# Where an attention kernel's filler matmuls stand, and when transposed activations leave PSUM

## The chip, the cores and the metric

The kernel runs on one core of a Trainium2 chip. The metric is the device time of one execution in microseconds (us). The same execution leaves a trace of every instruction on each engine: TensorE (PE, with its weight loads shown apart as PEld), VectorE (DVE), ScalarE (ACT), GpSimd (POOL) and SyncE (SP), whose queue issues the DMAs.

## The reference

One layer of an encoder over 1024 tokens of width 1024, all in float32:

```
h = x @ w_in                                # qa ka va qb kb vb ga gb
y_a = banded softmax attention(qa, ka, va, rel_bias) @ w_proj_a    # 8 heads of 64, branch A
y_b = stick-breaking attention(qb, kb, vb) @ w_proj_b              # 8 heads of 64, branch B
mix = (sigmoid(ga + b_a) * y_a + sigmoid(gb + b_b) * y_b) @ w_out
x   = LN(alpha * x + mix)
g, u = split(x @ w_ffn_in)
out = LN(alpha * x + (silu(g) * u) @ w_ffn_out)
```

Branch A lets a 64-token chunk attend to itself and the 8 chunks before it. Branch B computes weights beta_ts * prod(1 - beta_tj) with beta = sigmoid(q.k / 8), strictly causal. The tokens are held in reversed order, so that both masks reach forward.

## The kernel before, in words

Every product that needs float32 accuracy is made of three matmuls: an operand is split into a high part (ACT casts it) and a low part (DVE or POOL subtracts the high part from the raw value), and high*high, high*low and low*high are summed in PSUM. `split` (L110, L111) is the pair of instructions that does it. The large projections run as seven half-size products in place of eight (`pair_steps`, `product`).

The stages in order of time: the input projections (to 333 us), the 16 attention heads (333 to 643 us; 0 to 7 are branch A, 8 to 15 branch B), the gated branch projections and the output projection (to 773 us), the first layer norm with its transposes (in the same stretch), the feed-forward network (from 773 us).

A framework places the instructions. It takes the order in which the program issues them as a priority and gives each engine the first one that its own estimate of durations holds ready; only instructions tied with `keep_in_program_order` keep their order on their engine. Buffers are drawn from pools: `slot` gives one of a few 128x1024 tiles of a tag, `bank` one of the eight PSUM banks (`mm` 2, `sc` 2, `tr` 3, `pv` 1). A buffer comes free when its last reader is done, and whoever wants it waits for that.

**The heads.** A loop over `vsteps` has 12 steps (`pos`) for each head: 8 for the first half of the queries (`g` = 0), 4 for the second. A step emits, in this order: the score units that `LEAD` calls for (`wunits`; a score unit is one 128-query block; in branch A, step 2 emits the first block of the *next* head, in two cuts of 320 columns), postponed work (`later`), the step's transposes of weights (`turn`, L807, evacuated by `split` into `pt`), half of its filler matmuls, the product with V of the step two or three back (`mult`, L820 and L821, into the one `pv` bank), and the rest of its fillers. At the end of each half head ACT copies the `pv` bank out (L839); only then can the next half's first `mult` start.

In branch A a score block is reduced by DVE out of its `sc` bank (L738), exponentiated by ACT (L744), divided by POOL (L749) and only then transposed. In branch B, ACT takes two sigmoids out of the `sc` bank (L776, L777), DVE scans (L779, L782) and POOL multiplies (L784).

**The fillers.** 480 matmuls that do not depend on the heads' chains are dealt out among the steps: the gates 10 to 15 (48 matmuls each, `gate`, L598) and branch A's output projection (192, `yAps`, L896). `FILL` says how many each head gets (18 in heads 0 to 6, 34 in head 7, 38 to 40 in branch B), `AHEAD` is 8 at the start; `goal` is the running count and `fill_until` emits fillers up to it. While gate i runs, the weights of gate i+1 are split once, at the start of its second half (`half_way`): one ACT cast of 128x1024 (L549) and one POOL subtraction of 128x1024 (L550), both tied.

**The transposed x.** After the first layer norm (`layer_norm`, `norm_1`), `x1_operands(hf)` transposes half of the tokens: per `kt` two PSUM banks of four 128x128 transposes each (L1178). Each bank is read three times: ACT casts the high half (L110), DVE subtracts for the low half (L111), ACT copies the raw value (L1188 for hf 0, L1197 for hf 1). `x1_operands(0)` comes after token tile 4 of the second column half of the output projection (`ops`, L117, L118 and L120, 24 matmuls a tile); `x1_operands(1)` runs between the two products of the first feed-forward column block (`plainhl`, `plainhr`).

Of the kernel before, what the change touches and what calls it, by code (L numbers as in the profile page):

```python
# [11 lines left out]
F32 = mybir.dt.float32  # L12
F32R = mybir.dt.float32r
AF = mybir.ActivationFunctionType
ALU = mybir.AluOpType
# [20 lines left out]
LAG = 2  # L36
LEAD = ((6, 8, 9, 9, 10, 10, 11, 11, 12, 12, 13, 13), (7, 8, 9, 9, 10, 10, 11, 11, 12, 12, 13, 14))

FILL = (18, 18, 18, 18, 18, 18, 18, 34, 40, 40, 39, 39, 40, 38, 38, 38)
AHEAD = 8  # L40


# [6 lines left out]
def hybrid_trunk_kernel(ctx: ExitStack, tc, x, xt, w_first, w_v, w_in, b_gate, rel_bias, w_proj,  # L49
# [59 lines left out]
    def split(dst_h, dst_l, src):  # L109
        return (nc.scalar.copy(dst_h, src),  # L110
                nc.vector.tensor_tensor(dst_l, src, dst_h.bitcast(F32), ALU.subtract))  # L111
# [426 lines left out]
    def begin_w(srcs, name, raw, hl, lo_eng, in_turn=False):  # L538
        r = raw(f"wr_{name}")
        srcs = srcs if isinstance(srcs, list) else [(slice(0, 1024), srcs)]  # L540
        for cs, src in srcs:
            ins = dma(r[:, cs], src)
            if in_turn:
                tc.keep_in_program_order(ins)

        def end(tied=False):
            hi = hl(f"wh_{name}", F32R)
            lo = hl(f"wl_{name}", F32R)
            for ins in (nc.scalar.copy(hi, r),  # L549
                        lo_eng.tensor_tensor(lo, r, hi.bitcast(F32), ALU.subtract)):  # L550
                if tied:
                    tc.keep_in_program_order(ins)
            return hi, lo
        return end

# [35 lines left out]
    def gate(i, w, half_way, freed=None):  # L591
        gt = slot("gt", f"gate{i}")
        acc = [bank("mm", f"gps{i}_{hf}") for hf in range(1 if freed is None else 2)]

        def part(hf, k):
            ks = slice(k * P, (k + 1) * P)
            for j, (lw, rx) in enumerate(((w[0], xh), (w[0], xl), (w[1], xh))):
                mm(acc[hf], lw[:, ks], rx[k][:, (LO, HI)[hf]], start=(k == j == 0),  # L598
                   stop=(k == KT - 1 and j == 2))
                yield 1.0  # L600

        def take(hf):
            nc.scalar.copy(gt[:, (LO, HI)[hf]], acc[hf])

        if freed is None:
            for hf in range(2):
                if hf:
                    acc.append(bank("mm", f"gps{i}_1"))
                    half_way()
                for k in range(KT):  # L610
                    yield from part(hf, k)
                take(hf)
        else:
            half_way()
            for k in range(6):
                for hf in range(2):
                    yield from part(hf, k)
                freed(k)
            for hf in range(2):
                for k in (6, 7):  # L620
                    yield from part(hf, k)
                    if k + hf == 7:
                        freed(7)
                take(hf)
                freed(6 + 2 * hf)
        dma(g_dr[i], gt)
# [226 lines left out]
        return steps  # L853


    def fill_all():
        w = first_w
        got = []
        for i in range(first_gate, 15):
            end = begin_gate(i + 1, nc.gpsimd)  # L860
            yield from gate(i, w, lambda: got.append(end(True)))
            w = got.pop()
        end = begin_proj(0, 0)
        ends = {}

        pieces = []

        def freed(k):
            if k < 4:
                ends[k] = begin_y(k)  # L870
            if 1 < k < 6:
                ends[k - 2](LO)
                pieces.append(lambda: ends[k - 2](HI))
            elif k > 5:
                pieces.pop(0)()

        yield from gate(15, w, lambda: None, freed)
        w = end()
        gates = {0: begin_gA(0)}
        for cc in range(4):  # L880
            if cc < 3:
                end = begin_proj(0, cc + 1)
            for j in range(2):
                c = 2 * cc + j
                t = gates.pop(c)
                squash(t, c, 0)
                if c < 7:
                    gates[c + 1] = begin_gA(c + 1)
                for hf, cs in enumerate((LO, HI)):
                    acc = bank("mm", f"yAps{c}_{hf}")  # L890
                    if j == 1 and hf == 0 and cc < 3:
                        got.append(end())
                    for k in range(4):
                        ks = slice(j * HW + k * P, j * HW + (k + 1) * P)
                        for n, (lw, rx) in enumerate(((w[0], yh), (w[0], yl), (w[1], yh))):
                            mm(acc, lw[:, ks], rx[k][:, cs], start=(k == n == 0),  # L896
                               stop=(k == 3 and n == 2))
                            yield 1.0
                        if k == 1 and pieces:
                            pieces.pop(0)()  # L900
                    nc.vector.tensor_tensor(t[:, cs], acc, t[:, cs], ALU.mult)
                if c < KEEP:
                    dma(m_dr[c], t)
                else:
                    kept[c] = t
                if c == 0:
                    end_y = begin_y(4)
                elif c < 3:
                    end_y((LO, HI)[c - 1])
            if cc < 3:  # L910
                w = got.pop()
# [94 lines left out]
    for si, (hd, g, st, box) in enumerate(vsteps):  # L1006
        hidx, pos = si // nhead, si % nhead
        if hidx < 14 and pos == 8:
            load_qk(heads[hidx + 2])
            if hidx < 6:  # L1010
                later.append([3, heads[hidx + 2]["end_bias"]])
        if pos == 4:
            if hidx < 15:
                load_v(heads[hidx + 1])
            else:
                next_w = begin_proj(1, 3)()
                end_11, end_21 = (begin_wo(name, raws, "xt")
                                  for name, raws in (("11", ("qs", "kh")), ("21", ("kl", "v"))))
        if hidx == 15 and pos == 10:
            end_11()  # L1020
        early = hd["br"] == 0 and st == LAG - 1 and len(pend) == LAG
        if early and g == 1:
            pend.pop(0)()
        while wi < min(hidx * 8 + LEAD[hd["br"]][pos], len(wunits)):
            wunits[wi]()
            wi += 1
        if si == 0:
            goal += AHEAD
            heads[1]["end_bias"](False)
            fill_until(goal)  # L1030
        if st == 0:
            steps_of[(hidx, g)] = value_steps(hd, g, box)
        turn, mult = steps_of[(hidx, g)][st]
        for item in list(later):
            item[0] -= 1
            if item[0] == 0:
                later.remove(item)
                item[1]()
        turn()
        last = goal  # L1040
        goal += FILL[hidx] / nhead
        fill_until(0.5 * (last + goal))
        if early and g == 0:
            pend.pop(0)()
        pend.append(mult)
        wait = hd["br"] == 0 and st == LAG
        while len(pend) > LAG + wait:
            pend.pop(0)()
        fill_until(goal)
# [118 lines left out]
    ops_1 = {p: [] for p in range(1, 8)}  # L1168
    x1raw, x1low, ops_21 = [], [], []

    def x1_operands(hf, acc_t):

        for kt in range(4):
            tps = []
            for k in (kt, kt + 4):
                tp = bank("tr", f"x1ps{hf}_{k}")
# [6 lines left out]
            if hf == 0:  # L1183
                raw = slot("op", f"x1raw{kt}")
                for i in range(2):
                    o = slot("xt", f"x1A1{i}_{kt}", F32R)
                    split(o[:, LO], o[:, HI], tps[i])
                    nc.scalar.copy(raw[:, (LO, HI)[i]], tps[i])  # L1188
                    ops_1[1 + i].append((o[:, LO], o[:, HI]))
                x1raw.append(raw)  # L1190
            else:

                low = slot("kp", f"x1low{kt}")
                for i, (o, to) in enumerate(((cycle(QKV, f"x1A21_{kt}", F32R), ops_21),
                                             (slot("pt", f"x1A22_{kt}", F32R), ops_1[4]))):
                    split(o[:, LO], o[:, HI], tps[i])
                    nc.scalar.copy(low[:, (LO, HI)[i]], tps[i])  # L1197
                    to.append((o[:, LO], o[:, HI]))
                x1low.append(low)
        if hf == 0:  # L1200
# [26 lines left out]
    def left_f(f):  # L1227
        prep_left(Wf[f], f"f{f}", w_ffn_in[f], "bw" if f == 2 else "op")
# [139 lines left out]
    for hf, cs in enumerate((LO, HI)):  # L1368
        for tt in range(4, 8):
# [17 lines left out]
                    right_f(1)  # L1387
            if hf == 1:
                norm_1(tt)
                if tt == 4:  # L1390
                    x1_operands(0, acc_t)
        if hf == 0:
            left_f(2)

    first_h = []

# [177 lines left out]
```

## Time and profile before

| | us |
|---|---|
| median of 3 runs | 1425.95 (1424.87 to 1426.73) |
| the profiled execution's own time | 1425.8 |
| its span, first to last instruction | 1424.0 |
| PE busy, as the profile counts it | 1412.3 |
| DVE / ACT / POOL busy | 1054.5 / 683.0 / 245.9 |

The granted TensorE clock was 0.999 over the span. A matmul's record is longer than the distance to the next one, because matmuls are pipelined: records of 0.39 us start 0.227 us apart. So PE's busy share says little about small waits, and they are read from the distances between starts, and from the idle time in front of the weight loads (PEld).

### The profile page before, as it was taken

To read this page: it belongs to the slowest core of one execution; us is meant where nothing else is said; L and a number is where in the kernel's file an instruction comes from. 1 tells how busy PE (TensorE), PEld (TensorE's weight loads), DVE (VectorE), ACT (ScalarE), POOL (GpSimd) and SP (SyncE) were. 2 spreads that over 40 slices of the span, in tenths; PEclk is the share of its full clock that TensorE was granted. 3 is DMA by queue.
4 is the path that set the end of the run, shared out by engine and by line. 5 is a ranking of instruction groups with operands and counts; after the bars stand their busy time and mean duration, and the time that the engine had idled before them with its cause. 6 is when DMAs were issued, how large, how long until landed. Compare 5 with 4: busy or idle time off the path is not lost.

```text
span 1424.0 us, 19039 instructions
## 1 busy us (share of the span) xinstructions
PE 1412.3 (99%) x6672; PEld 1172.8 (82%) x6672; DVE 1054.5 (74%) x1669; ACT 683.0 (48%) x1188; POOL 245.9 (17%) x313
## 2 busy tenths in 40 slices
PE   9999999999999999999999999999999999999997
PEld 7888888888888888888888888888888888888886
DVE  8866657635777778878988947776777656978767
ACT  6444444555778788774423624444444433212201
POOL 0000000002555779750001000000000000100014
PEclk9999999999999999999999999999999999999999
DMA  7486478856676468755651224443444458787602
GB/s 255 159 295 223 163 251 311 294 183 212 213 222 199 135 228 296 249 196 198 231 198 69 74 75 163 148 148 135 150 159 163 148 192 280 281 312 238 204 15 104
DMA packets 104974, 276.54 MB, mean 194 GB/s; under 512 B 10400, under 2 KB 26784, under 8 KB 104880
## 3 DMA queue, kind: packets, MB, share of 16 engines
q1 hardware_dynamic: 104880, 275.35, 55.9%
q8 instruction: 52, 0.85, 0.3%
q14 instruction: 42, 0.34, 0.1%
HBM read 179.33 MB, written 92.30 MB: 191 GB/s over the span
## 4 chain that ended last, share of the span: by engine, by line
PE 93%; DVE 4%; ACT 2%; issue 1%; DMA 0%; POOL 0%; DVEq 0%; ACTq 0%; SPq 0%
PE sxf L180 16%; PE sxp L180 9%; PE szf L180 8%; PE dx L1496 6%; PE v L482 5%; PE szp L180 5%; PE gps L598 4%; PE syf L180 4%; PE dz L1496 3%; PE yAps L896 3%; PE syp L180 2%; PE tp_b L807 2%; PE ops L1343 2%; PE tp_a L807 2%; PE plain L348 2%; PE fpswh_h L118 2%
## 5 line engine op out<-in xcount | busy, mean ns | idle before, releaser
L784 POOL TENSOR_TENSOR w_b<-w_b,kp_b 128x511 f32<-128x511 f32 (+3 forms) x96 | 96.1, 1017 | 24.9 <-DVE kp_b L779 17.1
L1452 POOL TENSOR_TENSOR wdyt<-wdyt 128x512 f32<-128x512 f32 x8 | 11.2, 1405 | 512.5 <-DVE wdgt L1451 492.0
L779 DVE TENSOR_TENSOR_SCAN kp_b<-kp_b,ident_ps 128x512 f32<-128x512 f32 (+2 forms) x64 | 56.5, 884 | 23.3 <-ACT kp_b L776 22.4
L776 ACT ACTIVATE kp_b<-sc_b 128x512 f32<-128x512 f32 (+3 forms) x96 | 48.4, 505 | 30.7 <-PE sc_b L696 27.4
L180 PE MATMUL szf<-x1S63h,wcf 128*128 128x512 f32 x168 | 55.1, 389 | 0.0
L111 DVE TENSOR_TENSOR pt_b<-tp_b,pt_b 128x512 fp32r<-128x512 f32 (+1 forms) x96 | 50.0, 544 | 6.9 <-ACT pt_b L110 6.3
L719 POOL MEMSET bias<- 64x64 f32 x2 | 0.3, 144 | 313.4 <-ACT bias L715 313.4
L1427 DVE TENSOR_TENSOR x<-dx,x 128x512 f32<-128x512 f32 x64 | 43.3, 685 | 14.7 <-PE dx L1496 14.6
L111 DVE TENSOR_TENSOR sl<-h,sl 128x512 fp32r<-128x512 f32 x56 | 38.3, 685 | 19.5 <-ACT sl L110 19.5
L749 POOL TENSOR_SCALAR w_a<-w_a,st_a 128x640 f32<-128x640 f32 (+2 forms) x64 | 42.3, 666 | 57.3 <-PE sc_a L696 23.8
L110 ACT CAST sl<-h 128x512 fp32r<-128x512 f32 x56 | 34.7, 619 | 35.3 <-PE syf L180 17.1
L110 ACT CAST pt_b<-tp_b 128x512 fp32r<-128x512 f32 (+1 forms) x96 | 47.5, 505 | 8.0 <-PE tp_b L807 7.6
L744 ACT ACTIVATE w_a<-w_a,st_a 128x640 f32<-128x640 f32 (+2 forms) x64 | 44.8, 702 | 13.5 <-DVE st_a L738 12.2
L1156 POOL TENSOR_TENSOR mv<-mv,neghalf 128x1 f32<-128x1 f32 x16 | 11.9, 744 | 222.1 <-DVE mv L1155 222.0
L1274 ACT ACTIVATE h<-sxf 128x512 f32<-128x512 f32 x21 | 12.5, 597 | 77.3 <-PE sxf L180 77.3
L777 ACT ACTIVATE w_b<-sc_b 128x511 f32<-128x511 f32 (+3 forms) x96 | 48.6, 506 | 0.0
L111 DVE TENSOR_TENSOR pt_a<-tp_a,pt_a 128x512 fp32r<-128x512 f32 (+1 forms) x96 | 44.9, 485 | 4.8 <-ACT pt_a L110 3.1
L807 PE MATMUL tp_b<-ident,w_b 128*128 128x128 f32 x288 | 47.8, 273 | 0.4 <-DVE pt_b L111 0.3
L110 ACT CAST pt_a<-tp_a 128x512 fp32r<-128x512 f32 (+1 forms) x96 | 39.1, 432 | 11.0 <-PE tp_a L807 10.8
L807 PE MATMUL tp_a<-ident,w_a 128*128 128x128 f32 x240 | 43.2, 275 | 1.0 <-POOL w_a L749 0.4
L807 PEld LDWEIGHTS tp_b<-ident,w_b 128*128 128x128 f32 x288 | 35.6, 140 | 9.6 <-PE sc_b L696 1.3
L598 PE MATMUL gps<-xl,wh_g 128*128 128x512 f32 x96 | 43.0, 448 | 0.0
(1787 smaller groups left out, 4814.3 us busy)
## 6 DMA issues: line engine op xcount, KB each, us to landing
s_dr<-sl SPq DMA_DIRECT2D x112, 256.0 KB, 2.3
sd<-s_dr SPq DMA_DIRECT2D x56, 512.0 KB, 4.7
wLf<-in_w_ffn_in_dram SPq DMA_DIRECT2D x22, 512.0 KB, 4.5
wRf<-in_w_ffn_in_dram SPq DMA_DIRECT2D x22, 512.0 KB, 3.6
v_dr<-vc SPq DMA_DIRECT2D x16, 512.0 KB, 3.2
qs<-q_dr SPq DMA_DIRECT2D x16, 512.0 KB, 6.9
kh<-k_dr SPq DMA_DIRECT2D x16, 512.0 KB, 6.1
kl<-k_dr SPq DMA_DIRECT2D x16, 512.0 KB, 6.9
```

What stands on the lines that cost most here:

```text
L110: return (nc.scalar.copy(dst_h, src), nc.vector.tensor_tensor(dst_l, src, dst_h.bitcast(F32), ALU.subtract))
L111: nc.vector.tensor_tensor(dst_l, src, dst_h.bitcast(F32), ALU.subtract))
L180: mm(acc, lw[:, ks], rx, start=(first and kt == i == 0), stop=(kt == 3 and i == 2), skip_group_check=not first)
L482: mm(accs[j], a, b, start=(first and kt == n == 0), stop=(kt == 3 and n == 2), skip_group_check=True)
L598: mm(acc[hf], lw[:, ks], rx[k][:, (LO, HI)[hf]], start=(k == j == 0), stop=(k == KT - 1 and j == 2))
L744: nc.scalar.activation(s[:, 0:w], s[:, 0:w], AF.Exp, bias=st[:, m:m + 1], scale=-1.0, accum_out=st[:, 2:3])
L776: nc.scalar.activation(kp[:, c0:e], sc[:, 0:n], AF.Sigmoid, scale=-1.0)
L777: nc.scalar.activation(be[:, m0:e], sc[:, m0 - c0:n], AF.Sigmoid)
L779: nc.vector.tensor_tensor_scan(kp[:, 0:e], kp[:, 0:e], ident_ps()[:, 0:e], 0.0, ALU.mult, ALU.add)
L784: nc.gpsimd.tensor_tensor(be[:, m0:e], be[:, m0:e], kp[:, m0 - 1:e - 1], ALU.mult)
L807: tr(tp[:, (qb - lo_q) * P:(qb - lo_q + 1) * P], wt[qb - q0][:, (kb - qb) * P:(kb - qb + 1) * P], ident)
L1496: mm(acc, a, b, start=(first and i == n == 0), stop=(i == n - 1 == 1), skip_group_check=not first)
```

## The change

- In branch A's heads, step 2 emits fillers up to half a matmul over the running goal before its score unit (the next head's first block); the step's later marks are unchanged.
- In head 7, the last of branch A, steps 3 and 4 each raise the goal by 2. `FILL` gives heads 8 to 11 one filler less each. The sum stays 480.
- The split of the next gate's weights is done in two pieces of 512 columns: the first at `half_way`, the second after the third `k` of the gate's second half, nine fillers later.
- In `x1_operands` ACT copies the raw value out of PSUM first, and the high and low halves are then made from that copy in SBUF.
- `x1_operands(0)` is spread: `kt` 0 at the end of the first column half, `kt` 1 and 2 after token tile 4 of the second, `kt` 3 after token tile 5.

```diff
-FILL = (18, 18, 18, 18, 18, 18, 18, 34, 40, 40, 39, 39, 40, 38, 38, 38)
+FILL = (18, 18, 18, 18, 18, 18, 18, 34, 39, 39, 38, 38, 40, 38, 38, 38)
...
-        def end(tied=False):
+        def end(tied=False, rest=None):
             hi = hl(f"wh_{name}", F32R)
             lo = hl(f"wl_{name}", F32R)
-            for ins in (nc.scalar.copy(hi, r),
-                        lo_eng.tensor_tensor(lo, r, hi.bitcast(F32), ALU.subtract)):
-                if tied:
-                    tc.keep_in_program_order(ins)
+
+            def part(cs):
+                for ins in (nc.scalar.copy(hi[:, cs], r[:, cs]),
+                            lo_eng.tensor_tensor(lo[:, cs], r[:, cs], hi[:, cs].bitcast(F32),
+                                                 ALU.subtract)):
+                    if tied:
+                        tc.keep_in_program_order(ins)
+
+            if rest is None:
+                part(slice(0, 1024))
+            else:
+                part(LO)
+                rest.append(lambda: part(HI))
             return hi, lo
...
                 for k in range(KT):
                     yield from part(hf, k)
+                    if hf and k == 2 and rest:
+                        rest.pop()()
                 take(hf)
...
-            yield from gate(i, w, lambda: got.append(end(True)))
+            yield from gate(i, w, lambda: got.append(end(True, rest)))
...
+        if hidx == 7 and pos in (3, 4):
+            goal += 2
+        if hd["br"] == 0 and pos == 2:
+            fill_until(goal + 0.5)
         while wi < min(hidx * 8 + LEAD[hd["br"]][pos], len(wunits)):
...
-    def x1_operands(hf, acc_t):
+    def x1_operands(hf, acc_t, kts=range(4)):
-        for kt in range(4):
+        for kt in kts:
...
-                    split(o[:, LO], o[:, HI], tps[i])
-                    nc.scalar.copy(raw[:, (LO, HI)[i]], tps[i])
+                    part = raw[:, (LO, HI)[i]]
+                    nc.scalar.copy(part, tps[i])
+                    split(o[:, LO], o[:, HI], part)
...
-                    split(o[:, LO], o[:, HI], tps[i])
-                    nc.scalar.copy(low[:, (LO, HI)[i]], tps[i])
+                    part = low[:, (LO, HI)[i]]
+                    nc.scalar.copy(part, tps[i])
+                    split(o[:, LO], o[:, HI], part)
...
-                if tt == 4:
-                    x1_operands(0, acc_t)
+                if tt < 6:
+                    x1_operands(0, acc_t, ((1, 2), (3,))[tt - 4])
         if hf == 0:
             left_f(2)
+            x1_operands(0, acc_t, (0,))
```

More of the change, by code (lines that the diff above doesn't have):

```diff
@@ L853, in value_steps @@
         return steps
+    rest = []
     def fill_all():
```

## The prediction, made before the changed kernel ran

> **What bounds the kernel now.** I read the page's shares and chain first, then the chain in order of time, then the busy times by stretch, and last the timeline around every place where PE starts late.
>
> ```profile
> PE 1412.3 (99%) x6672; PEld 1172.8 (82%) x6672; DVE 1054.5 (74%) x1669; ACT 683.0 (48%) x1188; POOL 245.9 (17%) x313
> PE 93%; DVE 4%; ACT 2%; issue 1%; DMA 0%; POOL 0%; DVEq 0%; ACTq 0%; SPq 0%
> 27.87 2.72 PE sxp L180 x12
> 388.00:404.00 16.00, 15.46 (x97) 13.26 (x95) 11.95 (x46) 13.27 (x33) 10.93 (x12) 1.00 0.68 202
> 452.00:462.00 10.00, 9.46 (x51) 7.17 (x50) 7.80 (x14) 9.38 (x23) 5.27 (x10) 1.00 0.90 269
> 484.00:506.00 22.00, 22.00 (x125) 18.85 (x124) 17.38 (x25) 17.67 (x42) 15.27 (x18) 1.00 0.61 196
> ```
>
> PE is the bound: 99% busy and 93% of the chain. The third line sets the unit: 12 matmuls in 2.72 us, so PE starts one of 512 columns every 0.227 us. The change neither adds nor removes a matmul or a transpose, and it issues no other DMA. So it can pay only where PE starts later than its unit, and it costs only where it makes PE do so. The stretches (stretch, length, then busy PE, PEld, DVE, ACT, POOL, then clock and DMA) say where to look: around the change of branches ACT is busy 9.38 of 10 us, while in branch B every other engine has a fifth or more of its time free (ACT 17.67 of 22).
>
> **First scores of a head (one filler moved ahead of them).** The stretch around step 2 of head 3:
>
> ```profile
> 388.04 0.27 PE L821 MATMUL pv_a<-pt_a,v 128*128 128x128 f32 x1
> 388.24 0.51 ACT L744 ACTIVATE w_a<-w_a,st_a 128x256 f32<-128x256 f32 x1 [0.51 <-DVE st_a L738]
> 388.26 0.42 PE L695 MATMUL sc_a<-kh,qs 128*128 128x320 f32 x1
> 388.52 0.31 PE L696 MATMUL sc_a<-kl,qs 128*128 128x320 f32 x1
> 388.67 0.31 PE L695 MATMUL sc_a<-kh,qs 128*128 128x320 f32 x1
> 389.50 0.58 ACT L839 COPY yt<-pv_a 128x512 f32<-128x512 f32 x1
> 389.68 0.47 PE L598 MATMUL gps<-xl,wh_g 128*128 128x512 f32 x1
> 390.13 0.19 PEld L820 LDWEIGHTS pv_a<-pt_a,v 128*128 128x128 f32 x1 [0.28 <-ACT yt L839]
> ```
>
> The `mult` at 388.04 has 128 columns (a quarter of the unit, 0.06), yet the score starts 0.22 later: 0.16 lost, and 0.11 more on the next distance (0.26 at 388.26 to 388.52, where the same pair takes 0.15 at 388.52 to 388.67). I take 0.11 as the refill after any wait. A filler of 0.227 fits into that 0.27. But PE waits again at 390.13, for ACT's copy of the `pv` bank, which ends at 390.08 (389.50 + 0.58). That copy is late because ACT stood idle 0.51 us until DVE's reduction at 388.24; none of this chain waits for the scores that the filler now precedes. The moved filler comes from the same stretch, between 388.67 and 390.13. So PE saves 0.27 at the scores and waits that much longer at 390.13. Value 0. Best end: the planner finds other matmuls for the second hole, 0.27 in each of seven heads, 1.9 us. Worst end: the scores come after the filler without having been late, one refill of 0.11 in each of eight heads, 0.9 us of loss. I take 0 because the copy's row is the later end.
>
> **Gate weights in two pieces.** Five weights are split during the heads; the places where it shows:
>
> ```profile
> 354.81 1.06 ACT L549 CAST wh_g<-wr_g 128x1024 fp32r<-128x1024 f32 x1
> 356.41 0.33 PE L821 MATMUL pv_a<-pt_a,v 128*128 128x128 f32 x1
> 356.75 0.42 PE L695 MATMUL sc_a<-kh,qs 128*128 128x320 f32 x1
> 398.38 2.39 POOL L550 TENSOR_TENSOR wl_g<-wr_g,wh_g 128x1024 fp32r<-128x1024 f32 x1
> 400.76 2.24 POOL L749 TENSOR_SCALAR w_a<-w_a,st_a 128x640 f32<-128x640 f32 x3
> 402.39 0.33 PE L807 MATMUL tp_a<-ident,w_a 128*128 128x128 f32 x1 [0.42 <-POOL w_a L749]
> 461.46 1.29 POOL L784 TENSOR_TENSOR w_b<-w_b,kp_b 128x512 f32<-128x512 f32 x1
> L110 ACT CAST sl<-h 128x512 fp32r<-128x512 f32 x56 | 34.7, 619 | 35.3 <-PE syf L180 17.1
> ```
>
> POOL's 2.39 us stands in front of three divisions, and a transpose waits 0.42 for one of them. A half costs 1.2 (half of 2.39) to 1.29 (the 512-wide row), so the divisions start 1.1 us sooner and that wait goes: 0.42 and most of a refill, 0.5. After the ACT cast at 354.81 the scores come 0.34 after the `mult` where head 3 had 0.22: 0.12, and some more behind it; I count 0.3. The other three weights I count at 0.2 together. Against it stand the second pieces: ACT gets two casts of 0.619 for one of 1.06, 0.18 more each time, and that of the second weight falls, nine fillers on, about half a head later, into the next head's ACT chain shown above: 0.4 lost. Sum: 0.5 + 0.3 + 0.2 - 0.4 = 0.6 gained; ends 1.3 gained (a refill at every place, nothing lost) and 0.9 lost (five times 0.18 on the path and nothing gained).
>
> [...]
>
> **The change of branches (four fillers sooner).**
>
> ```profile
> 453.50 1.28 ACT L776 ACT_TABLE_LOAD   x1
> 455.57 0.40 PE L598 MATMUL gps<-xl,wh_g 128*128 128x512 f32 x1
> 455.93 0.44 PE L695 MATMUL sc_b<-kh,qs 128*128 128x384 f32 x1
> 456.21 0.34 PE L696 MATMUL sc_b<-kl,qs 128*128 128x384 f32 x1
> 456.39 0.39 PE L598 MATMUL gps<-xh,wl_g 128*128 128x512 f32 x1
> 456.91 0.50 PE L695 MATMUL sc_b<-kh,qs 128*128 128x512 f32 x1
> 457.25 0.40 PE L696 MATMUL sc_b<-kl,qs 128*128 128x512 f32 x1
> 457.61 0.39 PE L598 MATMUL gps<-xh,wh_g 128*128 128x512 f32 x1
> 458.41 0.66 PE L807 MATMUL tp_a<-ident,w_a 128*128 128x128 f32 x4 [0.41 <-DVE pt_a L111]
> ```
>
> ACT loads a table (1.28 us) and is behind from there on; PE waits for it directly or through DVE. The distances over the unit: 0.36 - 0.23 = 0.13; 0.28 where 384 columns take 0.17, 0.11; 0.52 - 0.23 = 0.29; 0.34 - 0.23 = 0.11; 0.80 - 0.23 = 0.57. Together 1.2 us. Four fillers are 0.91 us of work, emitted in the two steps that hold these waits; I take 0.8, since the last wait will keep a rest and a refill. Ends: 1.1 (refills gone too) and 0 (the fillers go where PE isn't waiting). What pays for it, four fillers fewer in heads 8 to 11, I cost at nothing: their cover is gone, but in the stretch from 484 PE has no idle time in the profile and ACT, DVE and POOL each have at least 4 of 22 us free. If that cover were needed, each would cost 0.227 and a refill, 1.3 in all, and the part would lose 0.5. With the fillers move what their generator emits between them, the gate's copy out of PSUM on ACT and its store and the next weight's load on SP: up to four matmuls sooner in both queues, 0.9 us, with a whole gate of 48 matmuls until anyone needs them; nothing.
>
> **Transposed x.**
>
> ```profile
> 747.42 1.05 ACT L110 CAST wlf2h<-wLf 128x1024 fp32r<-128x1024 f32 x1
> 752.49 1.57 ACT L110 CAST x1A<-x1ps 128x512 fp32r<-128x512 f32 x3 [4.03 <-PE x1ps L1178]
> 754.33 0.40 PE L120 MATMUL ops<-wh_o,mo 128*128 128x512 f32 x1
> 754.95 0.58 ACT L1188 COPY x1raw<-x1ps 128x512 f32<-128x512 f32 x1 [0.90 <-DVE x1A L111]
> 755.59 0.66 PE L1178 MATMUL x1ps<-ident,acc 128*128 128x128 f32 x4 [0.87 <-ACT x1raw L1188]
> PEld x1ps L1178 <- ACT x1raw L1188: 1.9, 4, 1.3
> PEld x1ps L1178 <- ACT x1low L1197: 0.6, 2, 0.3
> ```
>
> PE starts a transpose at 755.59 that could have started at 754.56 (754.33 + 0.227): 1.03 us, for want of a bank, because the raw copy that frees one runs last, after ACT's casts and DVE's subtraction. With the copy first, a bank is free 0.58 us after its transposes, and `kt` 0 is out of the way a token tile (24 matmuls, 5.4 us) sooner, in a stretch where ACT stands idle 4.03 us before 752.49; its banks are free once the cast at 747.42 is through, at the latest. So this wait goes. The five other waits of the weight loads there are 1.2 us (1.9 + 0.6 - 1.3), partly under the matmul before; I count half, 0.5 to 0.6. The part's sum: 1.5 gained. Ends: 2.0 (everything, with a refill) and 0.5 (a new wait of half a microsecond at `kt` 1 and 2, which still need four banks where three exist). The high half now comes one ACT instruction (0.6) later, but nobody takes it for several microseconds; DVE's and ACT's counts stay, only their source is SBUF.
>
> **The sum.** 0 + 0.6 + 0.8 + 1.5 = 2.9 us. The profiled execution took 1425.8 (its span of 1424.0 and 1.8 around it), 0.15 under the median, so: 1425.8 - 2.9 = 1422.9, against the median 1423.05. I say 1423.0. A measurement of this kernel tells about 0.2%, 2.85 us, from no change; the bounds of "same" are 1423.1 and 1428.8, and my forecast stands on the lower one.
>
> **Rivals.**
> 1. *The first scores pay too.* The planner fills the second hole as well: 1.8 us more, 1421.2. For it: the fillers are the one thing on PE that is always ready. Against it: the `pv` copy's row. 0.22.
> 2. *The halves cost.* ACT's 0.18 is on the path five times, 0.9 lost in place of 0.6 gained: 2.9 - 1.5 = 1.4, 1424.5. [...] For it: the ACT chain is what ends the wait in every branch A head. Against it: in 388 to 404 ACT is idle 2.7 of 16 us. 0.18.
> 3. *The fillers stay where they were.* They are not tied, the marks are only priorities, and the planner fits them by its own times. Then only the transposed x pays: 1424.4. 0.08.
> 4. *Slower: scores and transposes get interleaved.* In head 0 the planner did this:
>
> ```profile
> 341.00 0.41 PE L695 MATMUL sc_a<-kh,qs 128*128 128x320 f32 x1
> 341.36 0.44 PE L807 MATMUL tp_a<-ident,w_a 128*128 128x128 f32 x2
> ```
>
> A score's high matmul, then transposes that wait, then its low one: 0.36 where 0.15 is due. Twice or three times a head that is 0.4 to 0.7 us. If the filler ahead of the scores turns the seven other heads into this order, 7 x 0.7 = 4.9 is lost, less 2.9: 1427.9. It decides from about five heads on (5 x 0.7 = 3.5). Against it: the heads after the first keep the program's order. 0.12.
>
> **How the numbers follow.** Forecast 0.40, its own range 1421.7 to 1424.2. Below 1423.1 lie 0.26 of the forecast's 0.40, nearly all of rival 1 (0.21) and a little of rival 2 (0.01): faster 0.48. Slower: 0.11 of rival 4, 0.01 of rival 2: 0.12. The rest, 0.40, is same. The range runs from 1420.3 (rival 1 with the best ends of two parts) to 1427.0 (half of rival 4's price).
>
> **What would show it.** Right: no wait for x1raw above 0.2 us in front of a transpose; between 454 and 459 distances of PE over its unit of 0.4 us in all; no transpose waiting 0.4 for a POOL division; the waits on `pv` at step 3 of branch A longer by about 0.2, those on the scores gone. Wrong: those `pv` waits shorter (rival 1), PE waits in heads 8 to 11, new waits nine fillers after each first piece (rival 2), or scores cut apart by transposes (rival 4).

## The result, and the profile after

| | before | after |
|---|---|---|
| median of 16 runs each, us | 1425.67 | 1423.07 (1421.99 to 1423.53) |
| ratio, 95% interval | | 0.9979 (0.9972 to 0.9987) |
| the profiled execution's own time / its span | 1425.8 / 1424.0 | 1423.1 / 1421.3 |
| profiled execution: first score to last matmul | 1083.22 | 1079.96 |

The change gains 2.6 us (by the interval 1.9 to 4.0) where 2.9 was forecast. In the profiled execution the part that it touches became 3.26 shorter; the first score came 0.62 later (333.71 against 333.09), in a stretch that the change leaves alone. In the twelve kernels of the experiments, which share that stretch, the first score comes at 332.6 to 334.6, so the 0.62 is chance from one execution to the next.

The page of the changed kernel, the busy times and the chain:

```profile
PE 1409.4 (99%) x6672; PEld 1171.5 (82%) x6672; DVE 1054.4 (74%) x1669; ACT 682.8 (48%) x1193; POOL 247.0 (17%) x318
PE 94%; DVE 2%; ACT 2%; DMA 1%; issue 1%; DVEq 0%; POOL 0%; SPq 0%; ACTq 0%
```

The counts are what the diff says: as many matmuls, five more instructions on ACT and on POOL. The busy sums of DVE and ACT hardly move, and PE's falls by 2.9, like the time as a whole, so none of them tells where the gain was made. DVE's share of the chain falls from 4% to 2%.

The account that does resolve it is a sum of lateness. For every matmul I take the distance to the next start, less what its columns need (0.227 us for 512, in proportion for fewer, as the trace shows them back to back: 0.18 for 384, 0.15 for 320 and 0.06 for 128 between 388 and 391 us of the changed kernel), and add up over a stretch:

| PE late, us | before | after | forecast |
|---|---|---|---|
| branch A up to the first score of branch B | 11.91 | 10.34 | -0.6 (halves) and 0 (first scores) |
| the 10 us of the change of branches | 1.59 | 1.22 | -0.8 for this line and the next |
| the rest of branch B | 8.61 | 8.06 | |
| transposed x, first half | 1.34 | 0.17 | -1.5 for this line and the next |
| transposed x, second half (40 us) | 0.41 | 0.77 | |

The five lines together lose 3.30, which agrees with the 3.26. The absolute sums depend on what a transpose is taken to need; the differences between kernels hardly do. How far such a line can be trusted is seen in four kernels with the same heads (before, x1_alone, x1_copy and x1_spread, below): the rest of branch B 8.60 to 8.64, branch A 11.36 to 12.11.

**First scores**, step 2 of head 3 in the timeline of the changed kernel:

```profile
388.15 0.28 PE L832 MATMUL pv_a<-pt_a,v 128*128 128x128 f32 x1
388.26 0.44 PE L607 MATMUL gps<-xh,wl_g 128*128 128x512 f32 x1
388.35 0.51 ACT L755 ACTIVATE w_a<-w_a,st_a 128x256 f32<-128x256 f32 x1 [0.52 <-DVE st_a L749]
388.54 0.31 PE L706 MATMUL sc_a<-kh,qs 128*128 128x320 f32 x1
388.69 0.30 PE L707 MATMUL sc_a<-kl,qs 128*128 128x320 f32 x1
389.60 0.48 PE L607 MATMUL gps<-xl,wh_g 128*128 128x512 f32 x1
389.60 0.58 ACT L850 COPY yt<-pv_a 128x512 f32<-128x512 f32 x1
390.24 0.50 PE L831 MATMUL pv_a<-pt_a,v 128*128 128x512 f32 x1 [0.16 <-ACT yt L850]
```

The filler stands at 388.26, and the score follows 0.28 later, 0.05 over the unit. But ACT still waits for DVE's reduction as before (idle 0.52 before 388.35, 0.51 in the kernel before), its `pv` copy ends at 390.18 (389.60 + 0.58), and the `mult` starts 0.64 after the filler in front of it: 0.41 late, where it was 0.22 late before (390.13 - 389.68 - 0.23).

**Gate weights**, the place in head 3 where a division kept a transpose waiting:

```profile
395.47 0.63 ACT L551 CAST wh_g<-wr_g 128x512 fp32r<-128x512 f32 x1
398.03 1.30 POOL L552 TENSOR_TENSOR wl_g<-wr_g,wh_g 128x512 fp32r<-128x512 f32 x1
399.29 1.59 POOL L760 TENSOR_SCALAR w_a<-w_a,st_a 128x640 f32<-128x640 f32 x2
401.25 0.60 PE L818 MATMUL tp_a<-ident,w_a 128*128 128x128 f32 x4
401.61 0.48 PE L607 MATMUL gps<-xh,wl_g 128*128 128x512 f32 x1
403.04 0.61 ACT L551 CAST wh_g<-wr_g 128x512 fp32r<-128x512 f32 x1
```

The divisions follow 1.26 after the subtraction in place of 2.38, and the four transposes run in one piece. Behind the second cast, 7.6 us after the first, head 4, into whose chain it falls, is no later than head 3 with its 0.41: its first `mult` starts 0.39 late (405.54 - 404.92 - 0.23).

**Change of branches**:

```profile
455.47 0.34 PE L707 MATMUL sc_b<-kl,qs 128*128 128x384 f32 x1
455.96 0.50 PE L706 MATMUL sc_b<-kh,qs 128*128 128x512 f32 x1 [0.16 <-ACT w_b L788]
456.31 0.40 PE L707 MATMUL sc_b<-kl,qs 128*128 128x512 f32 x1
456.78 0.40 PE L607 MATMUL gps<-xh,wl_g 128*128 128x512 f32 x1
457.46 0.65 PE L818 MATMUL tp_a<-ident,w_a 128*128 128x128 f32 x4 [0.28 <-DVE pt_a L111]
```

Five late starts of 1.2 us became three: 0.32, 0.11 and 0.45, together 0.88.

**Transposed x**, first half:

```profile
746.50 1.07 ACT L1205 COPY x1raw<-x1ps 128x512 f32<-128x512 f32 x2
747.46 1.15 ACT L110 CAST x1A<-x1raw 128x512 fp32r<-128x512 f32 x2
750.87 1.93 PE L1195 MATMUL x1ps<-ident,acc 128*128 128x128 f32 x16
751.50 1.08 ACT L1205 COPY x1raw<-x1ps 128x512 f32<-128x512 f32 x2 [2.89 <-PE x1ps L1195]
752.56 0.49 PE L117 MATMUL ops<-wh_o,mo 128*128 128x512 f32 x1
```

Sixteen transposes (`kt` 1 and 2) run as one, and the next matmul comes 1.69 after the first of them: 0.106 for each. The wait of 0.87 for `x1raw` is gone.

### The profile page after: what moved, and what is told of

Same layout as the page of the kernel before. It is cut to its first block, busy times and chain, and to the rows that moved or that the text cites. A ratio compares the mean times of both kernels' runs of the same rounds, so it can differ in the third digit from the quotient of the medians.

```text
span 1421.3 us, 19039 instructions
## 1 busy us (share of the span) xinstructions
PE 1409.4 (99%) x6672; PEld 1171.5 (82%) x6672; DVE 1054.4 (74%) x1669; ACT 682.8 (48%) x1193; POOL 247.0 (17%) x318
## 4 chain that ended last, share of the span: by engine, by line
PE 94%; DVE 2%; ACT 2%; DMA 1%; issue 1%; DVEq 0%; POOL 0%; SPq 0%; ACTq 0%
PE sxf L180 16%; PE sxp L180 9%; PE szf L180 8%; PE dx L1516 6%; PE v L482 5%; PE szp L180 4%; PE gps L607 4%; PE syf L180 4%; PE dz L1516 3%; PE yAps L909 3%; PE ops L1362 3%; PE tp_b L818 2%; PE syp L180 2%; PE tp_a L818 2%; PE fpswh_h L120 2%; PE fpswh_h L117 2%
## 5 line engine op out<-in xcount | busy, mean ns | idle before, releaser
L607 PE MATMUL gps<-xh,wl_g 128*128 128x512 f32 x96 | 43.0, 448 | 0.0
```

## The experiments

The first four each do one part alone, from the kernel before.

**x1_alone**: both edits of `x1_operands` and nothing else. 

> The kernel before with only the transposed x changed (copied out of PSUM first, and spread); attention as before. Prediction's step: 1.5 us gained. What the changed kernel's trace says: the wait of 1.03 us for a bank goes, but the second half of x loses 0.36, so 0.8 us gained, with a wait of about 0.24 for the first feed-forward multiplication near 799 us. If the gain of the whole change sat in the attention stage, nothing is gained here.

Median 1425.22 against 1425.63, ratio 0.9998 (0.9990 to 1.0007). The first half's lateness falls from 1.34 to 0.17 and the second half's rises from 0.41 to 0.78. The waits of the weight loads between 735 and 815 us hold something new:

```profile
PEld syf L180 <- DVE h L1249: 0.5, 1, 0.5
```

**gate_alone**: the two pieces and nothing else. 

> The kernel before with only the gate weights split in two pieces. Prediction's step: 0.6 us gained, made of the wait for a POOL division at 402 us (0.42 idle, gone), 0.5 at the other places, and 0.4 lost at the second piece of the second weight. The changed kernel's trace says more: about 1.2 us, no loss at the second pieces. Rival 2 (the casts' fixed cost on ACT's path): up to 0.9 us lost.

Median 1424.86, ratio 0.9993 (0.9984 to 1.0001). Branch A's lateness is 10.08, the rest as before. Gone are 0.57 behind the first weight's cast (four late starts from 356.41 to 357.40 before), 0.64 at 402.39 and some smaller ones in heads 1 and 4; behind four of the five second pieces nothing new stands. Around the third weight's, PE is late by 0.39 where the kernel before has 0.11. Of this, 0.22 is a wait at 443.55 (with its refill) for a subtraction of DVE that began at 443.21, before ACT's second cast at 443.41; 0.06 and a refill, at 446.51, come 3 us behind that cast and may be its doing. No run separates that.

The 0.64 at 402.39 is not wholly the halves' either. In x1_spread, whose heads are those of the kernel before, the four transposes run in one piece without them:

```profile
401.67 0.68 PE L807 MATMUL tp_a<-ident,w_a 128*128 128x128 f32 x4
```

In x1_alone that start is 0.4 late, in x1_copy 0.6. Gone as well, and on no list of mine, is 0.39 at 398.06, a wait for DVE's `pt_a` and its refill that all four kernels with these heads have.

**first_alone**: one filler ahead of the first scores and nothing else. 

> The kernel before with only the filler ahead of each head's first scores. Prediction's step: 0, with the waits on the scores gone and those on the pv bank longer by about 0.2 in each of seven heads. Rival 1: up to 1.9 us gained, the pv waits as before. A loss of 0.9 us if the scores had not been late.

Median 1425.97, ratio 1.0003 (0.9994 to 1.0013). Branch A 11.60, inside what the same heads vary by. In most heads 0.16 in front of the scores goes and the wait in front of the first `mult` grows from 0.15 to 0.32. At the change of branches the five late starts are 1.0 in place of 1.2 (the third is 0.05 in place of 0.29), but another start, at 463.83, is later by as much.

**branch_alone**: the fillers of head 7 and `FILL` and nothing else. 

> The kernel before with only the four fillers moved to the change of branches. Prediction's step: 0.8 us gained, waits of PE between 454 and 459 us down from 1.2 to 0.4. The changed kernel's trace has 0.9 left there, so 0.3 to 0.4 gained. If heads 8 to 11 needed their fillers, up to 1.3 us lost in them.

Median 1425.55, ratio 1.0002 (0.9993 to 1.0011). The 20 us from the first score of branch B on are late by 1.71 (before 2.27), but 0.39 is lost again, at 501.69. At the places named in the prediction, three late starts of 1.1 in all (0.32, 0.11 and 0.68) are left of the 1.2. Two of these, and the place of the loss:

```profile
457.33 0.50 PE L695 MATMUL sc_b<-kh,qs 128*128 128x512 f32 x1 [0.15 <-ACT w_b L777]
458.82 0.66 PE L807 MATMUL tp_a<-ident,w_a 128*128 128x128 f32 x4 [0.52 <-DVE pt_a L111]
497.99 2.40 POOL L550 TENSOR_TENSOR wl_g<-wr_g,wh_g 128x1024 fp32r<-128x1024 f32 x1 [1.25 <-ACT wh_g L549]
500.36 2.54 POOL L784 TENSOR_TENSOR w_b<-w_b,kp_b 128x511 f32<-128x511 f32 x2
PEld tp_b L807 <- DVE pt_b L111: 0.7, 1, 0.7
```

(The last line is the waits of the weight loads from 490 to 510 us.) A whole subtraction lies in front of POOL's products at 500.36, and a transpose is late soon after. With the halves, in the changed kernel, that late start isn't there. That the subtraction causes it is read from the rows; no run separates it from the fillers that heads 8 to 11 lack.

The medians of the four parts alone move by -0.4, -0.8, +0.3 and -0.1, with intervals of about 1.2 us to each side. They neither confirm nor deny a sum of 2.6; the traces carry the attribution.

**x1_copy** and **x1_spread**: the copy first without the spreading, and the reverse. 

> The kernel before with only the raw copy first, x_operands not spread. Theory: the wait of 1.03 us for a bank in the first half shrinks to below 0.5 (a bank is free one ACT copy after its transposes), and the 0.24 near 799 us appears.

> The kernel before with only the first half's transposes spread, each bank read in the old order. Theory: spreading alone takes most of the 1.03 us, since two of the three banks suffice for kt 0 and two tiles of matmuls lie between the groups; a wait of up to 0.5 is left at kt 1 and 2, and nothing changes near 799 us.

One run each: 1425.65 and 1425.21. The copy alone takes the first half's lateness to 0.39 and has the second half's 0.79; the spreading alone leaves 1.13 and 0.39. With the spreading alone, which I expected to take most of the wait, it has only moved:

```profile
756.47 0.66 PE L1178 MATMUL x1ps<-ident,acc 128*128 128x128 f32 x4 [0.57 <-ACT x1raw L1188]
```

So the gain and the loss of this part are both the copy's; the spreading adds 0.2.

**hf1_mix**: in the changed kernel, the second half's `kt` 0 split out of PSUM as before, the rest copy first.

```diff
+                    if kt == 0:
+                        split(o[:, LO], o[:, HI], tps[i])
+                        nc.scalar.copy(part, tps[i])
+                    else:
...
```

> The changed kernel with the old order (cast, subtraction, then raw copy) for the first kt of the second half of x alone. Theory: DVE's row of work from the first transposes to the first feed-forward multiplication sets the end of that stretch, and the new order starts it one ACT copy later; with the old order for the first pair DVE starts 0.4 to 0.5 sooner, and the wait of 0.24 and its refill near 799 us go: 0.35 gained. Rival: the wait there comes from another engine and stays.

1422.51, 0.9972 (0.9962 to 0.9982). The wait for `h` stayed, so my remedy missed. The rows of the kernel before, of the changed kernel and of hf1_mix: ACT's first instruction, DVE's first, and `h`; in the second block also the matmul that waits for `h`, in the third DVE's wait for a copy.

```profile
779.08 1.56 ACT L110 CAST x1A<-x1ps 128x512 fp32r<-128x512 f32 x3 [14.74 <-PE x1ps L1178]
779.70 1.89 DVE L111 TENSOR_TENSOR x1A<-x1ps,x1A 128x512 fp32r<-128x512 f32 x3 [1.78 <-ACT x1A L110]
800.11 0.68 DVE L1247 TENSOR_TENSOR h<-plainhr_0f,gt 128x512 f32<-128x512 f32 x1
```

```profile
776.03 1.08 ACT L1215 COPY x1low<-x1ps 128x512 f32<-128x512 f32 x2 [15.14 <-PE x1ps L1195]
777.65 1.29 DVE L111 TENSOR_TENSOR x1A<-x1low,x1A 128x512 fp32r<-128x512 f32 x2 [2.78 <-ACT x1A L110]
798.04 0.69 DVE L1266 TENSOR_TENSOR h<-plainhr_0f,gt 128x512 f32<-128x512 f32 x1
798.79 0.73 PE L180 MATMUL syf<-x1A,wlf2h 128*128 128x512 f32 x2
```

```profile
776.92 1.08 ACT L110 CAST x1A<-x1ps 128x512 fp32r<-128x512 f32 x2 [15.14 <-PE x1ps L1195]
777.54 1.29 DVE L111 TENSOR_TENSOR x1A<-x1ps,x1A 128x512 fp32r<-128x512 f32 x2 [1.78 <-ACT x1A L110]
779.87 0.69 DVE L1237 TENSOR_TENSOR x1low<-x1low 128x512 f32<-128x512 f32 x1 [1.03 <-ACT x1low L1217]
798.93 0.68 DVE L1270 TENSOR_TENSOR h<-plainhr_0f,gt 128x512 f32<-128x512 f32 x1
```

In the mix DVE starts 0.62 after ACT in place of 1.62, and then stands idle 1.03 for a copy: the same 1.0 is paid one step on, and `h` comes 22.01 after ACT's first instruction in both, against 21.03 in the kernel before.

**hf1_old**: the second half wholly in the old order, everything else of the change kept. 

> The changed kernel with the second half of x read in the old order throughout (the first half copied first and spread). Theory: the wait near 799 us goes (0.24 and a refill), the small waits for a bank between 776 and 784 us come back (0.4 in all): no gain to 0.1 lost, and the first half's 1.03 us stays away.

One run: 1422.52. The second half's lateness is 0.43, the first half's stays 0.17, and from first score to last matmul it is 1079.66, 0.30 less than in the changed kernel. More than I expected: the small waits at the transposes, which I thought would come back, had never gone (0.27 in the kernel before, between 781 and 786 us; 0.28 in the changed kernel, between 776 and 780). x1_copy and x1_spread differ in the same way (0.79 and 0.39). The loss is settled by this: it is the second half's order.

**branch_3**: one filler more at each of the two steps of head 7 (`goal += 3`), two fewer in head 12. 

> The changed kernel with six fillers in place of four at the change of branches (three a step; head 12 gives two). Theory: PE's waits there (0.32, 0.11 and 0.45 in the changed kernel) end when ACT or DVE are done, so two fillers more take up to 0.45 of them if they are placed ahead of them. Rival: the planner puts them behind, and the waits stay as with four.

One run: 1423.25. The late transpose, and the longest new wait of branch B:

```profile
456.36 0.66 PE L818 MATMUL tp_a<-ident,w_a 128*128 128x128 f32 x4 [0.53 <-DVE pt_a L111]
PEld tp_b L818 <- PE sc_b L707: 1.5, 2, 1.1
```

The 10 us of the change are late by 1.23 (1.22 in the changed kernel): DVE's wait grew as the others shrank, so the two fillers more gain nothing there. The rest of branch B is late by 9.06, a loss of 1.0, most of it (0.8) in one start at 543.26, 90 us on; what causes it is not shown.

**pv_fill**: one filler more ahead of the first `mult` of each branch A head (step 3).

```diff
-        fill_until(0.5 * (last + goal))
+        fill_until(0.5 * (last + goal) + (1.25 if hd["br"] == 0 and pos == 3 else 0))
```

> The changed kernel with one filler more ahead of the first multiplication of each branch A head (step 3), taken from step 4. Theory: that multiplication waits for ACT's copy of the pv bank, which no matmul in the stretch delays, so its wait falls from 0.33 to about 0.1 in each of seven heads; 1.5 us gained, less what step 4 loses. Rival: the copy follows PE, the wait stays at 0.33, nothing gained, or 0.2 a head lost.

1420.68 (1420.42 to 1421.33), 0.9960 (0.9946 to 0.9973). The place in head 3, in that kernel:

```profile
387.26 0.51 ACT L755 ACTIVATE w_a<-w_a,st_a 128x256 f32<-128x256 f32 x1 [0.52 <-DVE st_a L749]
388.52 0.58 ACT L850 COPY yt<-pv_a 128x512 f32<-128x512 f32 x1
388.52 0.48 PE L607 MATMUL gps<-xl,wh_g 128*128 128x512 f32 x1
388.83 0.40 PE L607 MATMUL gps<-xh,wl_g 128*128 128x512 f32 x1
389.15 0.50 PE L831 MATMUL pv_a<-pt_a,v 128*128 128x512 f32 x1
```

The copy comes 1.26 after the exponential, as in the changed kernel (1.25): it does not follow the fillers. The second filler at 388.83 fills the hole, the `mult` is 0.09 late in place of 0.41, and branch A's lateness falls from 10.34 to 8.78.

**pv_no_first**: pv_fill without the filler ahead of the first scores. 

> The kernel of pv_fill without the filler ahead of the first scores (that one stays behind the scores, as before the change). Theory: one stretch per head with a fixed length; a filler moved inside it shifts the wait, one brought into it removes 0.2. So the waits on the scores (0.16 and a refill) are back in each of seven heads and those on the pv bank stay near 0; waits in branch A 0.3 to 0.8 us over pv_fill in all, far below the 1.9 that seven holes of 0.27 would give if the first filler counted by itself.

One run: 1421.82. The 0.16 in front of the scores is back in heads 2 to 6, and branch A is late by 9.48: by this the change's filler is worth 0.7, but only once the second hole is filled as well. The places show it; the size alone would be within what branch A varies by. At the change of branches the late starts are 0.34, 0.11 and 0.70, as in branch_alone, so this filler is worth another 0.2 there.

**best_two**: pv_fill and hf1_old together. 

> The changed kernel with the filler ahead of the first product with V of each branch A half head, and with the second half's transposes in the old order (ACT's and DVE's split out of PSUM first, the raw copy last); the first half keeps the copy first. My theory: the two edits lie in stages that do not touch (333 to 488 us and 773 to 815 us), so what each took off the lateness of PE alone adds: branch A 8.8 us as with the filler alone (10.3 in the changed kernel), the second half's 40 us 0.4 (0.8 in the changed kernel). From first score to last matmul 1078.1 us, 0.3 less than with the filler alone; a time about 0.3 under that kernel's 1420.7 (0.5 us of it is start-up chance), 1420.0 to 1420.9, and 0.995 to 0.997 of the kernel before. Rival: the 0.3 was one profile's chance and the second half's order is worth nothing; then from first score to last matmul 1078.4 and the second half's lateness stays near 0.8.

1420.37 (1420.09 to 1421.38) against 1425.87, 0.9964 (0.9951 to 0.9978). Branch A 8.54, second half 0.39, from first score to last matmul 1077.72. The two gains lie in different stages and add: 0.66 below pv_fill, of which 0.38 is the second half; the 0.24 of branch A is within what the same heads vary by. By the medians alone best_two and pv_fill are not told apart (1420.37 and 1420.68); every run of either is below every run of the changed kernel.

## Why the prediction was right

The total (2.9 forecast, 2.6 measured) is right, and so is the way to it: no engine's load, only late starts of PE. That the two are so near is in part luck: two terms were mis-sized in opposite directions (1.1 too small, 0.7 too large). Of the signs, the one on the change of branches did not come true: 0.4 in all was to be left between 454 and 459 us, and 0.88 was.

- **First scores, 0: right, with its reason.** The hole moved by the 0.2 foretold, in first_alone and in the change. Pv_fill shows the reason: the `pv` copy's time is set by ACT's chain (1.26 after the exponential, 1.25 in the changed kernel), and a filler just ahead of the `mult` closes the hole (0.09 late in place of 0.41). Rival 1 had the right place but not this change; the planner did not fill the second hole by itself.
- **Halves, 0.6: too small; some 1.7 by gate_alone** (10.08 against 11.75, the mean of the four kernels with the same heads; 1.3 to 2.0 against the single ones). The place behind the first cast gave 0.57 for my 0.3. The 0.5 at 402 comes and goes between kernels with the same heads (0.06 to 0.64); 0.39 at 398.06 and the small ones in heads 1 and 4 I had not listed. And the step that failed is the loss of 0.4 for the second piece of the second weight: none shows there.
- **Rival 2** fell, but for at most 0.2 us. The two casts do cost more than one: 0.18 by their records (0.63 and 0.61 against 1.06), but records of neighbours overlap (the copies of 746.50 end at 747.57, the casts behind them begin at 747.46), and back to back two casts out of SBUF take 1.15 (747.46 above) where one of 1024 columns takes 1.05 (747.42 before), so 0.1. Of the five times 0.18 at most the 0.2 at the third weight reached PE.
- **Change of branches, 0.8: the size was near, the place mostly wrong.** The 20 us from the first score of branch B on fell from 2.27 to 1.53, 0.74. The waits that I had named gave 0.34 of it (1.2 to 0.9), and most of that is not the four fillers': alone they take 0.1 there (branch_alone), and without the filler ahead of head 8's first scores, the last of the moved ones, 1.15 is left (pv_no_first). So the step that failed is that fillers emitted in the two steps fill the waits in them: the last wait is DVE's chain for `pt_a`, which the fillers did not shorten, and in branch_3 two more only lengthened it (0.53 in place of 0.28). The other 0.4 are three late starts between 464 and 473 us (0.13, 0.14 and 0.10) that my list did not have; they are gone in branch_alone too. The nothing at which I costed heads 8 to 11 held in the changed kernel: 0.18 less between 80 and 90 us after that first score, 0.1 more between 50 and 60. It did not hold in branch_alone, where 0.39 was lost in head 10 (at 501.69).
- **Transposed x, 1.5: too large; 0.8.** The first half gave 1.17: the wait of 1.03 and little more. The small waits for a bank, which I half counted with 0.5 to 0.6, stayed in the second half (0.27 before, 0.28 after). The other step that failed is that nobody takes the high half "for several microseconds": DVE, idle for 2.78 until the first cast, takes it at 777.65, 0.66 after that cast's start. Its row of work from there to `h` lasts 20.4 us with hardly a gap (779.70 to 800.11 before, DVE busy 20.31 of it; 777.65 to 798.04 after, 20.32) and had some 0.75 of slack (an estimate: 1.0 less 0.24); starting 1.0 later, it makes PE wait at 798.79 (0.24 and a refill of 0.11). That wait is of DVE on ACT, not on PSUM, and I had looked only at who waits for the banks.
- **Rivals 3 and 4** are excluded by the rows: the fillers stand where the program puts them, and scores are cut apart by transposes in head 0 alone, three times before and after.

## What to carry to other kernels

Where one engine is busy throughout, read the distances between its starts; here a filler took 0.16 in front of the scores and the wait in front of the next `mult` grew from 0.15 to 0.32 (first_alone), since the copy that ended that wait did not move (1.26 after the exponential before, 1.25 in the changed kernel); so follow the chain to an instruction whose time the fillers do not set (here the `pv` copy), and put a filler ahead of whoever waits for it. Before a copy is put ahead of a split to free a bank sooner, ask which engine reads the split next and how much slack its row of work has: the same edit gained 1.0 us (x1_copy) where no start of PE waited for DVE afterwards, and lost 0.4 where one did. Parts that change 0.5 us each can't be told apart by medians at 0.1%; one profile for each, read at the places that were named beforehand, can, if the place repeats: look at it in several kernels that should not differ there, as the wait at 402 us shows.

## What the runs showed that I had not expected

- Lateness repeats to 0.04 us in the rest of branch B over four kernels with the same heads (8.60 to 8.64), while branch A varies by 0.75 (11.36 to 12.11), some 0.5 of it in head 3 alone: the wait at 402 us.
- DVE subtracted as fast from a copy in SBUF as from PSUM: two of 512 columns in 1.29 us at 777.65 of the changed kernel (from `x1low`) and at 777.54 of hf1_mix (from `x1ps`). In the second half only the order on ACT cost time (0.77 late, 0.43 in hf1_old).
